# Spectra of the hyena filters in a two-layer trunk: 256 samples summed at 256 frequencies, and the same from even and odd samples at 128 frequencies

## The chip, the cores and the metric

One NeuronCore of one Trainium2 chip runs the whole kernel. The metric is the time of one execution on the device in microseconds (us); a profile gives the span from the first to the last instruction of one profiled execution.

## What is computed

The reference is a trunk of two layers over 256 tokens of 2048 channels in float32, with 256 context tokens. Layer 0 is attention (two kinds of heads) and a gated convolutional feed-forward part; layer 1 is a Hyena long convolution of order 2 and again a feed-forward part. Every sub-layer is preceded by an RMS norm with a scale and a shift that come from a conditioning vector (the modulation). What the change touches is the Hyena filters and the long convolution with them:

```python
hf = (a @ f_w3).reshape(L, HY_ORDER, 2, D_MODEL)          # a: a sine network of the position, L = 256
filt = hf * decay[:, None, None, :]

def _bidir_long_conv(u, h_fwd, h_bwd, d_skip):
    filt = concatenate([h_fwd, zeros((1, D)), h_bwd[:0:-1]], axis=0)
    filt = filt / sum(abs(filt), axis=0, keepdims=True)
    n = 2 * L
    y = irfft(rfft(u, n=n, axis=1) * rfft(filt, n=n, axis=0)[None], n=n, axis=1)[:, :L]
    return y + u * d_skip
```

There are two orders, so 2 x 2 x 2048 filters of 256 samples. They do not depend on the tokens.

## The kernel before, in words

Every large product is made of three matmuls (`mm3`, lines 319 to 322): both operands are split into a high part, rounded to the float32r type by ScalarE (L315 for weights, L325 for other tiles), and a low part, the difference by VectorE (L316, L326). TensorE (PE) computes high x high (L320), and the two mixed products (L321, L322, in the order in which they are called). Weights are read in tiles of 256 rows x 512 columns (512 KB), through a pool of 6 raw buffers and 3 pairs of split buffers; the DMAs are issued on SyncE's queue (SP).

**Order of the work.** The program is written as generators. `drive` (L300) steps a main stream and after each step gives shares of steps to background streams. A scheduler then sets the order of each engine's instructions from the order in which they were recorded and from priorities; an engine runs its instructions in that order.

**The start** (up to about 181 us). The scale and shift vectors of the first norm are products of the conditioning vectors with 33.5 MB of weights. `ada_block(g)`, g from 0 to 3, makes 512 columns of both (L871: PE reads the raw weights; L875 to L883 turn the sums into columns), and the first projection of the attention keys and values (label kv0) follows it block by block, since each block lets another quarter of the normed tokens be computed (`Normed.get`, L379). Beside them, `bg.step(START_RATE)` steps the generators `filter_net` and `filters` for the first two of four groups of 512 channels (`DCS`, L173).

**`filters`** (L526) makes, for each group of channels and each order, the samples (`samples`: L546 PE, L548 VectorE times the decay, L325/L326 split, L550 absolute values, L555 to L560 the norm) and then the spectra (`spectra`, L563). The samples' tile `layers` holds forward + backward and forward - backward; their cosine and sine sums are the two halves of a spectrum at the 256 frequencies f + 1/2. A sum over 256 samples at 128 frequencies takes two tiles of samples (tt) and so 2 x 3 matmuls of 128 x 512 into one bank; ScalarE scales the bank into the tile `so` (L572); after both frequency tiles of a half a DMA on ScalarE's queue (L574) writes the half to memory. So each (order, channel group) has 24 matmuls, 4 ScalarE passes and 4 steps (`yield`). There are 8 of them: 4 in the start, 2 in the fill of the attention's output projection, 2 in that of the first down projection.

**The fills.** `fill` (L1091) runs the samples of one more channel group beside the last pass of a projection back into the stream. Then the kernel has to wait: the norm of the next sub-layer needs the sums of squares of the finished stream, by a chain of L352 (PE sums), L354 (VectorE), L331 and L332 (VectorE, first guess of a root), L334 to L344 (GpSimd, Newton steps), L360 (ScalarE), L361 (PE), L388 (VectorE), L393 (ScalarE), and only then the next sub-layer's matmuls. `main_done` and `fill_steps` (L1101, L1109) put the remaining steps of the spectra there: `GAP = 3, 5` steps before the chain is recorded and after it, and the rest of the steps (up to 40) after the first normed group. The chain runs at high priority. There are three such gaps: before the first feed-forward part (about 700 to 713 us), before the Hyena layer (about 1523 to 1536 us), both with fill, and before the second feed-forward part (about 1975 to 1985 us), without.

**The modulation of later sub-layers** is computed by VectorE during everything (L434, L436: 128 x 1024 products, from `araw` tiles through two buffers), so VectorE's queue now and then waits for such a DMA with other work behind it.

In the start the filters take their banks from a ring of two banks (6 and 7), in the fills from a ring of four.

## Time and profile before

| | |
|---|---|
| time, median of 3 runs | 2727.53 us (2714.11 to 2729.07) |
| span of the profiled execution | 2722.9 us; the profile gives no time outside it |
| TensorE (PE) busy | 2588.1 us, 95%, 19638 matmuls |
| VectorE (DVE) busy | 1931.1 us, 71%, 2581 instructions |
| ScalarE (ACT) busy | 1267.0 us, 47%, 1810 instructions |
| GpSimd (POOL) busy | 35.1 us, 1% |
| memory traffic | 639.97 MB, mean 235 GB/s |
| mean granted clock of TensorE | 0.986 of full speed |

A group of instructions of the page gives line, engine, operation, output <- inputs, shapes, count, then busy time and the mean of one in ns. Matmuls overlap (the next enters the array while the last one leaves), so the duration of one is longer than the distance between two. The chain that ended last consists of PE for 60% and of DMA for 18%, of which 16% are the `araw` transfers of the modulation.

### The profile page before, as it was taken

What the parts mean: (1) busy time and instruction counts of PE and PEld (TensorE: products, weight loads), DVE (VectorE), ACT (ScalarE), POOL (GpSimd) and SP (SyncE); (2) the same over time, 40 slices, a digit from 0 to 9 for tenths busy, and PEclk for the clock granted to TensorE, in tenths of its full rate; (3) what the DMA queues carried; (4) which work ended last, traced back from release to release, by engine and by line L of the source; (5) the groups of instructions that cost most, each with busy time, mean ns of one, the idle gap of its engine ahead of it and who ended that gap; (6) DMA issues with size and microseconds to landing.
All of it is one profiled execution on the core that took longest, in us unless ns stands there. A gap on an engine that the chain in (4) does not pass through costs nothing.

```text
span 2722.9 us, 48064 instructions
## 1 busy us (share of the span) xinstructions
PE 2588.1 (95%) x19638; PEld 2371.2 (87%) x19638; DVE 1931.1 (71%) x2581; ACT 1267.0 (47%) x1810; POOL 35.1 (1%) x146
## 2 busy tenths in 40 slices
PE   6999999989999999999899999998989999999999
PEld 2567776678889999999898899998989999999999
DVE  6557668688877777768778778888777655556564
ACT  3542235655544343445444555554454444445543
POOL 0000001000000000000000000000000000000000
PEclk8999999999999999999999999999989999999999
DMA  8887785278698989878897865555579666666664
GB/s 309 311 308 240 229 273 182 86 236 267 217 307 273 300 283 312 270 244 292 292 302 261 274 196 179 170 178 186 169 233 310 203 195 192 194 193 195 194 208 141
DMA packets 282628, 639.97 MB, mean 235 GB/s; under 512 B 19783, under 2 KB 19880, under 8 KB 282408
## 3 DMA queue, kind: packets, MB, share of 16 engines
q1 hardware_dynamic: 280104, 628.53, 71.8%
q10 hardware_dynamic: 2304, 8.39, 0.8%
q8 instruction: 153, 2.51, 0.4%
q14 instruction: 67, 0.55, 0.1%
HBM read 624.25 MB, written 12.58 MB: 234 GB/s over the span
## 4 chain that ended last, share of the span: by engine, by line
PE 60%; DMA 18%; DVE 13%; issue 5%; ACT 2%; POOL 1%; SPq 1%; DVEq 0%; ACTq 0%; POOLq 0%
DMA araw_ada<-ada_w 16%; PE ps_proj L322 6%; PE ps_proj L321 6%; PE ps_proj L320 5%; DVE aacc_ada L436 4%; PE ps_hy L322 3%; PE ps_hy L321 3%; PE ps_hy L320 3%; DVE wlo_proj L316 2%; DMA raw_proj<-wd 1%; PE ps_ada L871 1%; PE ps_kv L320 1%; PE ps_kv L322 1%; PE ps_kv L321 1%; PE ps_ada L320 1%
## 5 line engine op out<-in xcount | busy, mean ns | idle before, releaser
L436 DVE SCALAR_TENSOR_TENSOR aacc_ada<-araw_ada,slat,aacc_ada 128x1024 f32<-128x1024 f32 x300 | 384.7, 1282 | 236.9 <-DMA araw_ada<-ada_w 236.3
L322 PE MATMUL ps_proj<-ph,wlo_proj 128*128 128x256 f32 x1408 | 391.6, 280 | 18.2 <-DVE wlo_proj L316 18.1
L320 PE MATMUL ps_proj<-ph,whi_proj 128*128 128x256 f32 x1408 | 391.5, 279 | 3.7 <-ACT whi_proj L315 2.2
L315 ACT CAST whi_proj<-raw_proj 128x1024 fp32r<-128x1024 f32 x240 | 251.3, 1052 | 302.3 <-PE ps_proj L321 273.6
L321 PE MATMUL ps_proj<-pl,whi_proj 128*128 128x256 f32 x1408 | 390.7, 278 | 1.3 <-DVE pl L326 1.3
L316 DVE TENSOR_TENSOR wlo_proj<-raw_proj,whi_proj 128x1024 fp32r<-128x1024 f32 x240 | 291.9, 1221 | 116.6 <-ACT whi_proj L315 116.3
L322 PEld LDWEIGHTS ps_proj<-ph,wlo_proj 128*128 128x128 f32 x1408 | 264.6, 189 | 24.7 <-DVE wlo_proj L316 22.3
L320 PEld LDWEIGHTS ps_proj<-ph,whi_proj 128*128 128x128 f32 x1408 | 265.4, 189 | 7.4 <-ACT whi_proj L315 2.9
L321 PEld LDWEIGHTS ps_proj<-pl,whi_proj 128*128 128x128 f32 x1408 | 266.1, 189 | 3.0 <-DVE pl L326 2.3
L320 PE MATMUL ps_hy<-hhi,whi_hy 128*128 128x256 f32 x768 | 215.8, 282 | 1.1 <-ACT hhi L393 1.1
L321 PE MATMUL ps_hy<-hlo,whi_hy 128*128 128x256 f32 x768 | 215.2, 280 | 0.6 <-DVE hlo L395 0.6
L322 PE MATMUL ps_hy<-hhi,wlo_hy 128*128 128x256 f32 x768 | 214.8, 280 | 0.0
L315 ACT CAST whi_hy<-raw_hy 128x1024 fp32r<-128x1024 f32 x96 | 100.8, 1059 | 115.3 <-PE ps_hy L321 104.9
L321 PEld LDWEIGHTS ps_hy<-hlo,whi_hy 128*128 128x128 f32 x768 | 146.3, 190 | 2.2 <-DVE hlo L395 0.8
L320 PEld LDWEIGHTS ps_hy<-hhi,whi_hy 128*128 128x128 f32 x768 | 144.9, 189 | 2.5 <-ACT hhi L393 1.3
L322 PEld LDWEIGHTS ps_hy<-hhi,wlo_hy 128*128 128x128 f32 x768 | 145.1, 189 | 0.8 <-DVE wlo_hy L316 0.7
L316 DVE TENSOR_TENSOR wlo_hy<-raw_hy,whi_hy 128x1024 fp32r<-128x1024 f32 x96 | 116.3, 1220 | 24.5 <-ACT whi_hy L315 24.1
L320 PE MATMUL ps_kv<-whi_kv,hhi 128*128 128x512 f32 x256 | 102.8, 402 | 9.0 <-ACT KTb L749 6.2
L322 PE MATMUL ps_kv<-whi_kv,hlo 128*128 128x512 f32 x256 | 101.7, 397 | 0.0
L321 PE MATMUL ps_kv<-wlo_kv,hhi 128*128 128x512 f32 x256 | 101.3, 396 | 0.0
L315 ACT CAST whi_kv<-raw_kv 128x1024 fp32r<-128x1024 f32 x40 | 41.9, 1051 | 101.8 <-PE ps_kv L322 82.2
L320 PE MATMUL ps_proj<-oh,whi_proj 128*128 128x256 f32 x256 | 75.0, 297 | 2.2 <-DVE hf L548 1.2
(9846 smaller groups left out, 7973.2 us busy)
## 6 DMA issues: line engine op xcount, KB each, us to landing
araw_ada<-ada_w SPq DMA_DIRECT2D x320, 512.0 KB, 5.1
raw_proj<-wd SPq DMA_DIRECT2D x176, 512.0 KB, 4.5
raw_hy<-hw_in SPq DMA_DIRECT2D x96, 512.0 KB, 4.6
raw_ada<-ada_w SPq DMA_DIRECT2D x46, 512.0 KB, 6.8
raw_kv<-w_in SPq DMA_DIRECT2D x40, 512.0 KB, 4.8
raw_q<-w_in SPq DMA_DIRECT2D x32, 512.0 KB, 4.6
raw_proj<-w_out SPq DMA_DIRECT2D x32, 512.0 KB, 4.8
raw_proj<-hw_out SPq DMA_DIRECT2D x32, 512.0 KB, 4.0
```

What stands on the lines that cost most here:

```text
L315: A.copy(hi, raw)
L316: V.tensor_tensor(lo, raw, hi, op=ALU.subtract)
L320: PE.matmul(o, lh, rh, start=first, stop=False, **kw)
L321: PE.matmul(o, lh, rl, start=False, stop=False, **kw)
L322: PE.matmul(o, ll, rh, start=False, stop=last, **kw)
L436: V.scalar_tensor_tensor(out=a, in0=raw, scalar=slat[:, kt:kt + 1], in1=a, op0=ALU.mult, op1=ALU.add)
L871: PE.matmul(pv[32 * q:32 * q + 32], sl[:, 2 * i + q], raws[q // 2][:, q % 2], start=i == 0, stop=i == 6, tile_position=(0, 32 * q))
```

## The change

Frequencies f (even, 0 to 254) are now paired with 255 - f instead of standing beside the odd ones in rising order. Samples are stored even ones first, then odd ones, so that a tile of samples is one parity. At frequency 255 - f the even samples give the same sum up to a sign and the odd samples the other sign. `spectra` therefore makes per half only two sums at 128 frequencies, over the even tile (`pe`) and the odd tile (`po`), and forms both frequency tiles as their sum and difference: ScalarE scales `pe` into a new tile `e`, VectorE makes two `scalar_tensor_tensor` passes from `po` and `e`. Only the first 128 frequencies stand in the table, so `k_fg` is 512 columns narrower and `split_const` loads and splits one piece less at each of the three calls of `filters`. A half is one step now, not two. The comments were taken out too, which is left out here, and three lines added ahead of `spectra`, so that L320 to L322 are L323 to L325 below, L352 is L355, L354 is L357, L361 is L364, L436 is L439, L871 is L877.

```diff
-    fo = np.concatenate([np.arange(0, L, 2), np.arange(1, L, 2)])[None, :]
+    fo = np.concatenate([np.arange(0, L, 2), L - 1 - np.arange(0, L, 2)])[None, :]
     t = np.arange(L)[:, None]
-    ph = np.pi * ((t * (2 * fo + 1)) % (2 * n)) / n
-    fmat = np.concatenate([np.cos(ph), np.sin(ph)], axis=1).reshape(2, P, 512).transpose(1, 0, 2).reshape(P, 1024)
+    eo = np.concatenate([np.arange(0, L, 2), np.arange(1, L, 2)])
+    ph = np.pi * ((eo[:, None] * (2 * fo[:, :P] + 1)) % (2 * n)) / n
+    fmat = np.concatenate([np.cos(ph), np.sin(ph)], axis=1).reshape(2, P, 2 * P).transpose(1, 0, 2).reshape(P, 512)
...
-        "k_tab": tab, "k_fg": fg, "k_z": np.ascontiguousarray(z.T),
-        "k_decay": np.ascontiguousarray(decay.reshape(2, P, D).transpose(1, 0, 2)),
+        "k_tab": tab, "k_fg": fg, "k_z": np.ascontiguousarray(z[eo].T),
+        "k_decay": np.ascontiguousarray(decay[eo].reshape(2, P, D).transpose(1, 0, 2)),
...
-        fh, fl = (t.rearrange("p (t f) -> p t f", t=2) for t in split_const(0, 1024, "f"))
+        fh, fl = (t.rearrange("p (t f) -> p t f", t=2) for t in split_const(0, 512, "f"))
...
                 so = q4([P, 2, 512], F32, "spo")
                 xh, xl = hl[2 * half], hl[2 * half + 1]
-                for f in range(2):
-                    p = ftag[0]()
-                    for tt in range(2):
-                        c = slice(half * T + f * P, half * T + (f + 1) * P)
-                        mm3(p, fh[:, tt, c], fl[:, tt, c], xh[:, tt], xl[:, tt], tt == 0, tt == 1)
-                    A.activation(so[:, f], p, AF.Copy, scale=1.0 / (2 * T))
-                    yield
+                c = slice(half * P, (half + 1) * P)
+                pe, po = ftag[0](), ftag[0]()
+                mm3(pe, fh[:, 0, c], fl[:, 0, c], xh[:, 0], xl[:, 0], True, True)
+                mm3(po, fh[:, 1, c], fl[:, 1, c], xh[:, 1], xl[:, 1], True, True)
+                e = s2([P, 512], F32, "se")
+                A.activation(e, pe, AF.Copy, scale=1.0 / (2 * T))
+                V.scalar_tensor_tensor(out=so[:, 0], in0=po, scalar=1.0 / (2 * T), in1=e, op0=ALU.mult, op1=ALU.add)
+                V.scalar_tensor_tensor(out=so[:, 1], in0=po, scalar=(half * 2 - 1) / (2 * T), in1=e, op0=ALU.mult,
+                                       op1=ALU.subtract if half else ALU.add)
+                yield
                 A.dma_start(spec[o][dc][:, 2 * half:2 * half + 2], so)
...
-    dh, dl = split_const(1024, 512, "d")
-    ih, il = split_const(1536, 512, "i")
+    dh, dl = split_const(512, 512, "d")
+    ih, il = split_const(1024, 512, "i")
```

With half the steps per spectrum the generators come to their ends earlier, and the scheduler sets another order. Three places follow.

**TensorE's order in the first gap, the last rows ahead of the sum of the norm (L361, now L364)**, before. `ps_fill` are the banks of the spectra, `ps_proj` with `ones` those of the norm:

```order
L320 MATMUL ps_fill_6001<-fhl_5683,fh_5478 128x512
L321 MATMUL ps_fill_6001<-fhl_5684,fh_5478 128x512
L322 MATMUL ps_fill_6001<-fhl_5683,fl_5479 128x512
L321 MATMUL ps_fill_6009<-fhl_5684,fh_5478 128x512
L322 MATMUL ps_fill_6009<-fhl_5683,fl_5479 128x512
L320 MATMUL ps_fill_6009<-fhl_5683,fh_5478 128x512
L321 MATMUL ps_fill_6009<-fhl_5684,fh_5478 128x512
L322 MATMUL ps_fill_6009<-fhl_5683,fl_5479 128x512
L361 MATMUL ps_proj_1292_5985<-s_5986,ones_67 128x128 x2
```

The same place with the change:

```order
L325 MATMUL ps_fill_5916<-fhl_5643,fl_5443 128x512
L355 MATMUL ps_proj_1301_5928<-ones_67,sqacc_4171 128x1
L355 MATMUL ps_proj_1301_5928<-ones_67,sq_5862 128x1
L355 MATMUL ps_proj_1301_5928<-ones_67,sq_5865 128x1
L355 MATMUL ps_proj_1301_5928<-ones_67,sq_5892 128x1
L355 MATMUL ps_proj_1301_5928<-ones_67,sq_5895 128x1
L355 MATMUL ps_proj_1301_5928<-ones_67,sqacc_4171 128x1
L355 MATMUL ps_proj_1301_5928<-ones_67,sq_5862 128x1
L355 MATMUL ps_proj_1301_5928<-ones_67,sq_5865 128x1
L355 MATMUL ps_proj_1301_5928<-ones_67,sq_5892 128x1
L355 MATMUL ps_proj_1301_5928<-ones_67,sq_5895 128x1
L364 MATMUL ps_proj_1306_5956<-s_5957,ones_67 128x128 x2
```

Before, 26 matmuls of spectra stood between the last sum of squares and L361; now none does: all 12 that are left in this gap stand ahead of the sums. In the second gap 3 stand behind the sums, where 22 stood, and 6 more of before, which stood among the Hyena layer's first matmuls, are gone.

**VectorE's order in the first gap, from the norm's first instruction (L354, now L357) to the first product with it (L388, now L391)**, before:

```order
L354 TENSOR_SCALAR t_5968<-ps_proj_1287_5957 128x2
L316 TENSOR_TENSOR wlo_ffn0.0_1313_6104<-raw_ffn0.0_1311_6101,whi_ffn0.0_1312_6103 128x1024
L331 TENSOR_SCALAR t_5971<-t_5968 128x2
L436 SCALAR_TENSOR_TENSOR aacc_ada_1405_6871<-araw_ada_1417_6968,slat_84,aacc_ada_1405_6871 128x1024
L332 TENSOR_SCALAR t_5970<-t_5971 128x2
L436 SCALAR_TENSOR_TENSOR aacc_ada_1405_6871<-araw_ada_1422_7007,slat_84,aacc_ada_1405_6871 128x1024
L388 TENSOR_TENSOR ht_6020<-xs_4199,ps_proj_1292_5985 128x256 x3
```

And with the change:

```order
L357 TENSOR_SCALAR t_5939<-ps_proj_1301_5928 128x2
L576 SCALAR_TENSOR_TENSOR spo_5900<-ps_fill_5902,se_5909 128x512
L334 TENSOR_SCALAR t_5942<-t_5939 128x2
L577 SCALAR_TENSOR_TENSOR spo_5900<-ps_fill_5902,se_5909 128x512
L335 TENSOR_SCALAR t_5941<-t_5942 128x2
L576 SCALAR_TENSOR_TENSOR spo_5914<-ps_fill_5916,se_5923 128x512
L577 SCALAR_TENSOR_TENSOR spo_5914<-ps_fill_5916,se_5923 128x512
L439 SCALAR_TENSOR_TENSOR aacc_ada_1415_6815<-araw_ada_1420_6849,slat_84,aacc_ada_1415_6815 128x1024
L439 SCALAR_TENSOR_TENSOR aacc_ada_1415_6815<-araw_ada_1427_6912,slat_84,aacc_ada_1415_6815 128x1024
L391 TENSOR_TENSOR ht_5964<-xs_4163,ps_proj_1306_5956 128x256 x3
```

Inside the norm's chain (up to L332, now L335) two passes of 128 x 1024 have given way to two of 128 x 512. In the second gap the two passes of 128 x 1024 there (both L436) give way to two of 128 x 512 in the same manner.

**TensorE's order in the last modulation block of the start** (L871, now L877: products with the raw weights), before:

```order
L871 MATMUL ps_ada_260_1110<-raw_ada_261_1111,sl 32x512
L320 MATMUL ps_filters_1091<-fhl_858,fh_293 128x512
L321 MATMUL ps_filters_1091<-fhl_859,fh_293 128x512
L322 MATMUL ps_filters_1091<-fhl_858,fl_294 128x512
L320 MATMUL ps_filters_1091<-fhl_858,fh_293 128x512
L321 MATMUL ps_filters_1091<-fhl_859,fh_293 128x512
L322 MATMUL ps_filters_1091<-fhl_858,fl_294 128x512
L871 MATMUL ps_ada_260_1110<-raw_ada_261_1111,sl 32x512
L871 MATMUL ps_ada_260_1110<-raw_ada_262_1113,sl 32x512 x2
```

And with the change:

```order
L884 MATMUL ps_ada_270_1092<-sel_109,adast_1090 128x2 x4
L877 MATMUL ps_ada_271_1101<-raw_ada_272_1102,sl 32x512 x2
L877 MATMUL ps_ada_271_1101<-raw_ada_273_1104,sl 32x512 x2
L323 MATMUL ps_ada_121_448<-whi_kv_275_1112,hhi_1028 128x512
L323 MATMUL ps_ada_122_449<-whi_kv_275_1112,hhi_1028 128x512
L323 MATMUL ps_ada_123_450<-whi_kv_275_1112,hhi_1042 128x512
L323 MATMUL ps_ada_124_451<-whi_kv_275_1112,hhi_1042 128x512
```

Of the 96 spectra matmuls of the start, 24 stood among the products of the second block, 24 of the third and 48 of the last; of the 48 that are left 15, 33 and none, the last of them ahead of the last block's first product.

## Rows read from the trace of the kernel before

**Rows 1.** Engines by stretch: length, busy (count) of PE, PEld, DVE, ACT, POOL; clock, DMA share, GB/s.
```profile
75.00:100.00 25.00, 25.00 (x124) 16.31 (x123) 10.74 (x22) 10.68 (x20) 0.00 (x0) 1.00 0.77 272
100.00:125.00 25.00, 24.54 (x125) 13.24 (x120) 11.47 (x24) 11.83 (x24) 0.00 (x0) 1.00 0.97 342
125.00:150.00 25.00, 24.14 (x128) 15.39 (x128) 11.15 (x24) 14.51 (x30) 0.00 (x0) 1.00 0.96 331
150.00:170.00 20.00, 18.87 (x84) 11.72 (x84) 6.44 (x10) 8.95 (x18) 0.00 (x0) 0.91 0.96 341
...
670.00:730.00 60.00, 54.29 (x359) 48.55 (x359) 50.91 (x95) 37.17 (x70) 2.92 (x10) 0.94 0.57 182
```

**Rows 2.** What SyncE's DMA queue waited for, 60 to 200 us: total, times, longest.
```profile
SPq L309 <- PE ps_ada L871: 69.6, 22, 9.2
```

**Rows 3.** Instructions on the spectra's banks: count, ns min/median/max, first and last start.
```profile
L320 PE MATMUL ps_filters<-fhl,fh x32: 389/397/507, 74.7 to 160.5; 128*128 128x512 f32 x32
...
L548 DVE TENSOR_TENSOR hf<-ps_filters,dec x16: 679/688/693, 38.3 to 127.2; 128x512 f32<-128x512 f32 x16
```

**Rows 4.** Order in time on PE in the start: start, duration, instruction. First, seventh from it.
```profile
80.36 0.40 PE L320 MATMUL ps_filters<-fhl,fh 128*128 128x512 f32 x1
...
81.75 0.40 PE L322 MATMUL ps_ada<-whi_kv,hlo 128*128 128x512 f32 x1
```

**Rows 5.** The same at the start's end: last modulation product, then kv0 matmuls.
```profile
161.29 1.06 PE L871 MATMUL ps_ada<-raw_kv,sl 128*32 128x512 f32 x8
...
165.74 0.63 PE L322 MATMUL ps_ada<-whi_kv,hlo 128*128 128x512 f32 x1
...
168.30 0.63 PE L322 MATMUL ps_ada<-whi_kv,hlo 128*128 128x512 f32 x1
```

**Rows 6.** Order in time on DVE in the first gap, the norm's chain.
```profile
704.50 0.16 DVE L354 TENSOR_SCALAR t<-ps_proj 128x2 f32<-128x2 f32 x1 [1.98 <-PE ps_proj L352]
...
705.79 1.28 DVE L436 SCALAR_TENSOR_TENSOR aacc_ada<-araw_ada,slat,aacc_ada 128x1024 f32<-128x1024 f32 x1
706.99 0.16 DVE L332 TENSOR_SCALAR t<-t 128x2 int32<-128x2 int32 x1
```

**Rows 7.** Order in time on PE in the first gap and behind it.
```profile
710.08 0.39 PE L322 MATMUL ps_fill<-fhl,fl 128*128 128x512 f32 x1
711.45 0.78 PE L361 MATMUL ps_proj<-s,ones 128*128 128x128 f32 x4 [0.98 <-ACT s L360]
...
715.22 0.41 PE L322 MATMUL ps_ffn0.0_1303_6039<-hhi,wlo_ffn0.0_1307_6044 128*128 128x256 f32 x1
...
718.42 0.32 PE L320 MATMUL ps_ffn0.0_1301_6037<-hhi,whi_ffn0.0_1309_6073 128*128 128x256 f32 x1
```

**Rows 8.** DVE in the second gap, the norm's chain.
```profile
1528.02 0.16 DVE L354 TENSOR_SCALAR t<-ps_proj 128x2 f32<-128x2 f32 x1 [1.72 <-PE ps_proj L352]
...
1530.62 0.16 DVE L332 TENSOR_SCALAR t<-t 128x2 int32<-128x2 int32 x1
```

**Rows 9.** PE behind the second gap: first and last of 6 late spectra matmuls.
```profile
1554.51 0.47 PE L320 MATMUL ps_fill<-fhl,fh 128*128 128x512 f32 x1 [0.47 <-DVE ht L388]
...
1555.74 0.39 PE L322 MATMUL ps_fill<-fhl,fl 128*128 128x512 f32 x1
```

**Rows 10.** PE in the third gap, without fill, and behind it.
```profile
1982.82 1.22 PE L361 MATMUL ps_proj<-s,ones 128*128 128x128 f32 x4 [5.03 <-ACT s L360]
...
1985.19 0.58 PE L320 MATMUL ps_ffn1.0_3360_20704<-hhi,whi_ffn1.0_3365_20710 128*128 128x256 f32 x1 [1.15 <-ACT hhi L393]
...
1991.59 0.32 PE L321 MATMUL ps_ffn1.0_3361_20705<-hlo,whi_ffn1.0_3368_20740 128*128 128x256 f32 x1
```

**Rows 11.** PE by stretches of 1 us there: length, busy (count), clock, DMA share, GB/s.
```profile
1978.00:1979.00 1.00, 0.00 (x0) 0.51 0.72 180
...
1990.00:1991.00 1.00, 1.00 (x7) 0.50 0.00 0
```

**Rows 12.** DVE in the start: the longest wait for a modulation tile.
```profile
158.53 1.28 DVE L436 SCALAR_TENSOR_TENSOR aacc_ada<-araw_ada,slat,aacc_ada 128x1024 f32<-128x1024 f32 x1 [11.61 <-DMA araw_ada<-ada_w]
```

## Prediction

> **What bounds the kernel now.** I read the engines' totals first: TensorE is busy for 95% of the span, so it is the engine whose work counts, but what an instruction less on it is worth has to be read where that instruction stands. The change takes 12 of 24 matmuls from each of 8 spectra. By the lists of the instructions on the spectra's banks [rows 3] 96 of the 192 stood in the start, the rest in the fills: in the out-projection and first down projection themselves, and in the two gaps behind these.
>
> In the start the windows [rows 1] show TensorE without a pause from 75 to 150 us, and DMA at 0.77 of its engines in the first 25 us and at 0.96 to 0.97 after that. SyncE's queue waits 22 times, 69.6 us in all, for TensorE to be done with a raw tile of the modulation [rows 2]. So both limits lie near each other: fewer matmuls free raw tiles sooner, the DMA runs ahead, and is then full itself. In the gaps VectorE, GpSimd and ScalarE make the root of the norm one after the other, and TensorE can only fill. VectorE's order in time [rows 6, 8] shows two passes on other data inside that chain; TensorE's order [rows 7, 9, 10] shows what follows the gap, and at which clock.
>
> **The sum.** It is made against the profiled execution, span 2722.9 us, for which the profile gives no time outside the span. The median of the runs, 2727.53, is 4.6 above it, and I add that at the end.
>
> **Start.** 48 matmuls go. One lasts 397 ns [rows 3], but they overlap: from the first to the seventh start of a run [rows 4] it is 81.75 - 80.36 = 1.39 us for six, 0.232 us each. 48 x 0.232 = 11.1 us less work for TensorE; that is the upper end. The DMA caps it: from 75 to 161 us the windows [rows 1] moved 25 x 272 + 25 x 342 + 25 x 331 + 11 x 341 kB/us, together 27.4 MB. At 342 kB/us throughout that takes 80.1 us, not 86: 5.9 can be had. I take this value, as the queue's waits [rows 2] show that TensorE, not memory, is what holds the transfers up in the first stretch, and the 0.97 that nothing holds them up after it. Against it stands the clock. The last block's products lose all spectra between them, so TensorE will pause there for tiles. The trace shows what follows pauses: behind the last product at 161.29 us, where the stretch's clock falls to 0.91 in the mean, the 6 spacings between the matmuls at 165.74 and 168.30 are 0.43 us each [rows 5], not 0.23. I add one more such stretch of 8 matmuls, 8 x 0.2 = 1.6. Start: -5.9 + 1.6 = **-4.3**; ends -11.1 and 0.
>
> The Trainium skill (page "TensorE: Matmul & The Clock Gate", section "Back-to-back issue gap") gives 131 ns for a matmul of 512 columns in a sustained stream of weight loads and matmuls. By it the 48 would be worth 6.3 us, not 11.1; the spacing in this trace is 232 ns [rows 4], so the measurement decides, and the DMA's cap lies below either.
>
> **First gap.** VectorE's chain from its first instruction at 704.50 to the root's guess at 706.99 is 2.49 us, since two passes of 128 x 1024, 1.28 each, stand in it [rows 6]. In the new order two of 128 x 512 stand there. The trace has no such `scalar_tensor_tensor`; the nearest row of that size and engine, a product of 0.688 us that reads a bank too [rows 3], is what I take. Its ends are 0.64, half of the 1.28, and 1.28 itself. 2.49 - 2 x 0.69 = 1.1 less. Ahead of the sums 12 spectra matmuls stand now for 10 before (36 in all, 26 behind): at most 2 x 0.23 = 0.5 us later, which I count as nothing, as VectorE's squares feed the sums meanwhile. Against that no matmul is left to run behind the sums, where 26 stood: the last of them ended at 710.5, 1 us before the norm's broadcast (L361) at 711.45 [rows 7]. TensorE will stand idle as in the third gap, where the clock is at 0.51 while it idles, the broadcast waited 5.03 us and took 1.22 where the first gap's took 0.78, and the clock is still at 0.50 at 1990 [rows 10, 11]. With fill the matmuls that take 0.41 reach from 715.22 to the first of 0.32 at 718.42 [rows 7], 3.2 us, half of which, 1.6, is lost. Without, they reach from 1985.19 to 1991.59 [rows 10], 6.4 us: 3.2 lost, and 0.4 on the broadcast. So the clock makes the gap 3.2 + 0.4 - 1.6 = 2.0 dearer. Sum: -1.1 + 2.0 = **+0.9**; ends -1.1 and +2.0.
>
> **Second gap.** The chain takes 2.60 us with two passes of 128 x 1024 in it [rows 8], so the same edit gives -1.2. Six spectra matmuls that stood late, behind the gap, waited 0.47 and took 6 x 0.23 [rows 9]: -1.9. Three matmuls of fill are left behind the sums of 22, and I take the first gap's 2.0 for the clock here too. Sum: -1.2 - 1.9 + 2.0 = **-1.1**; ends -3.1 and +2.0.
>
> **At nothing, with their cover.** 32 passes on VectorE at about 0.69 are 22 us. In the start VectorE is busy for 11 of 25 us, in the out-projection for 50.9 of 60 [rows 1], where 4 of them come; without that cover they cost 2.8. 16 scaling passes of as many columns leave ScalarE, which is busy for 11 to 15 of 25 us [rows 1] and not the bound either. Three times one constant piece (256 KB, a rounding, a subtraction) is not loaded; the two later ones lie beside TensorE's stream, the first is 0.256 MB, under 1 us of DMA at 342. The DMA that stores a half now follows VectorE's two passes on ScalarE's queue, with roundings of weights behind it; both banks of the start's ring of two are held for the same time. The two passes take 1.4 us a half, and 16 halves lie between 74.7 and 160.5 [rows 3], one in 5.4 us; I take 0, and what it costs when a pass is late is a rival.
>
> Total -4.3 + 0.9 - 1.1 = **-4.5**: span 2718.4, median 2723.0.
>
> **Rivals.** (A) *Everything goes through.* The transfers of the start speed up by as much as TensorE does, and the gaps, shorter by their chains, leave the clock as it was: -11.1 - 1.1 - 3.1 = -15.3, 2712.2 us. For it: SyncE's waits [rows 2]; against it: 0.97 [rows 1]. Chance 0.20.
>
> (B) *The clock takes all.* Every microsecond at half clock counts, idle or not: in the third gap 1978.0 to 1991.6, half of 13.6, is 6.8 [rows 10, 11], 3.2 more than the 3.6 I took, in both gaps; and the start's pause costs the 3.2 us of its cold row in full, twice the 1.6 [rows 5]. -4.5 + 6.4 + 1.6 = +3.5, 2731.0 us. For it: the third gap, at half clock from its middle until 1991.59 [rows 10, 11]. Against it: over half of these 13.6 us TensorE only waits for the chain, which does not run on its clock. Chance 0.10. The Trainium skill (same page, section "HAM oscillation — how this bites in real kernels") reckons the penalty of a throttled stretch as half of its time. By it this rival would be the likeliest; that only matmuls pay is my reading of the rows, and no run here shows yet which holds.
>
> (C) *Slower: VectorE's new passes stand behind a modulation tile.* Products of the modulation wait in VectorE's order for their transfer, once for 11.61 us [rows 12]. In the new order such a product stands ahead of a spectrum's passes at two places of the start. Before, only ScalarE released a spectrum's bank; now VectorE does, so the ring of two stops TensorE, and the store's issue holds up ScalarE's roundings. It decides if the wait is longer than the matmuls that TensorE still has ahead in its order. Both in full: 2 x 11.6 - 4.5 = +18.7, 2746.2 us. For it: the start's DMA is full, so such tiles come late; against it: the row stands at the very end of the start, and earlier waits are shorter. Chance 0.10.
>
> **How the numbers follow.** The forecast, 2723.0, has 0.60. A measurement of this kernel can tell some 0.5% from no change, 13.6 us of 2727.53. The forecast and B lie inside; A lies 1.7 us beyond the bound, and with a few of the forecast's own outer cases I give it 0.18 as faster; C is beyond the other, and a little of it falls short. Faster 0.18, the same 0.74, slower 0.08. The range: the ends of the terms are -11.1 - 1.1 - 3.1 = -15.3 and 0 + 2.0 + 2.0 + 2.8 = +6.8, so 2712.2 to 2734.3. The runs shown lie 15 us apart (2714.11 to 2729.07), so a median of a few may lie some 2 or 3 us off: 2709 to 2737. That takes in A and B and leaves out C, and little else.
>
> **What would show it.** Right: the last modulation product ends 4 to 6 us earlier, with DMA above 0.95 from 75 us on; the chain in the first gap is 1.4 us from L357 to L335, in the second also; the broadcast L364 comes after a pause of TensorE at half clock. Wrong: the start's end does not move (DMA or VectorE holds it), a spectrum's pass waits for a modulation tile while TensorE's matmuls on the other bank wait for it, or the pauses of the gaps leave the clock at 1.00.

## The result and the profile after the change

The changed kernel takes 2749.59 us (median of 4 runs, 2744.02 to 2753.70) where before takes 2726.52 (4 runs, 2714.11 to 2729.07): ratio 1.0096, 95% interval 1.0067 to 1.0125, that is 23 us between the medians and 26 by the ratio. The forecast was 2723.0, its range ended at 2737.0. The profiled execution has a span of 2742.2 us, 19.3 more than before's.

To see where, I read the starts of the same products in TensorE's order in time in both traces: the last kv0 product of the start, the first and last product of a projection, the first product behind a gap. The start ends at 191.2 us where it ended at 182.3; the out-projection takes 158.0 us instead of 152.1, the first gap 14.4 instead of 13.2, the down projection of the first layer 301.5 instead of 290.6, the second gap 15.7 instead of 13.8. So +8.9, +5.9, +1.2, +10.9 and +1.9; some 9.5 us come back in the other stretches, which move by as much between two traces of before. *Cold* below is TensorE at a granted clock of 0.50 (1.2 GHz) where it has 1.00 (2.4 GHz) otherwise.

**The start.** Windows of the changed kernel, columns as in [rows 1]:

```profile
75.00:100.00 25.00, 24.27 (x100) 13.92 (x101) 14.63 (x23) 11.39 (x21) 0.00 (x0) 0.93 0.77 266
100.00:125.00 25.00, 22.72 (x111) 11.95 (x110) 15.21 (x30) 11.28 (x23) 0.00 (x0) 1.00 0.87 314
125.00:150.00 25.00, 22.47 (x109) 12.19 (x109) 9.96 (x17) 9.67 (x21) 0.00 (x0) 1.00 0.86 319
150.00:170.00 20.00, 17.31 (x72) 8.00 (x72) 4.85 (x12) 2.22 (x4) 0.00 (x0) 0.74 0.73 254
```

DMA falls from 0.96 and more to 0.87, 0.86 and 0.73, and TensorE idles too. SyncE's queue, the instructions on the spectra's banks, and TensorE in the last block:

```profile
SPq L312 <- PE ps_ada L877: 65.5, 25, 9.8
```
```profile
L323 PE MATMUL ps_filters<-fhl,fh x16: 393/452/796, 72.9 to 136.2; 128*128 128x512 f32 x16
L576 DVE SCALAR_TENSOR_TENSOR spo<-ps_filters,se x8: 686/692/694, 83.4 to 137.1; 128x512 f32<-128x512 f32 x8
L577 DVE SCALAR_TENSOR_TENSOR spo<-ps_filters,se x8: 680/681/684, 84.0 to 137.7; 128x512 f32<-128x512 f32 x8
```
```profile
151.29 3.28 PE L877 MATMUL ps_ada<-raw_ada,sl 128*32 128x512 f32 x8 [2.88 <-DMA raw_ada<-ada_w]
155.25 1.87 PE L884 MATMUL ps_ada<-sel,adast 128*128 128x2 f32 x8 [0.69 <-ACT adast L881]
157.05 1.93 PE L877 MATMUL ps_ada<-raw_ada,sl 128*32 128x512 f32 x8
...
170.06 1.05 PE L884 MATMUL ps_kv<-sel,adast 128*128 128x2 f32 x8 [0.78 <-ACT adast L881]
```

The spectra's last sum starts at 136.2, not at 160.5 [rows 3]. Behind it TensorE has only modulation products and kv0 products, in lumps. From 143.2 it uses the loaded raw tiles in a row, then waits 2.88 us for the next, with DMA full, and turns cold: eight modulation products, four at a time, take 1.93 us (157.05) where they took 1.06 [rows 5]. From 161.7 to 166.6 twenty kv0 products run in one go; no raw tile comes free meanwhile, and DMA pauses. The two windows, columns as above:

```profile
148.00:152.00 4.00, 1.12 (x4) 0.18 (x4) 3.30 (x5) 2.01 (x6) 0.00 (x0) 0.78 1.05 394
164.00:168.00 4.00, 4.00 (x28) 2.32 (x29) 0.00 (x0) 0.00 (x0) 0.00 (x0) 1.00 0.18 68
```

SyncE still waits for TensorE, 65.5 us in all [rows 2: 69.6].

**The first gap.** VectorE and then GpSimd in order of time:

```profile
716.64 0.16 DVE L357 TENSOR_SCALAR t<-ps_proj 128x2 f32<-128x2 f32 x1 [1.73 <-PE ps_proj L355]
716.72 0.68 DVE L576 SCALAR_TENSOR_TENSOR spo<-ps_fill,se 128x512 f32<-128x512 f32 x1
717.31 0.16 DVE L334 TENSOR_SCALAR t<-t 128x2 int32<-128x2 int32 x1
717.38 0.69 DVE L577 SCALAR_TENSOR_TENSOR spo<-ps_fill,se 128x512 f32<-128x512 f32 x1
717.98 0.16 DVE L335 TENSOR_SCALAR t<-t 128x2 int32<-128x2 int32 x1
718.05 0.69 DVE L576 SCALAR_TENSOR_TENSOR spo<-ps_fill,se 128x512 f32<-128x512 f32 x1
...
719.24 2.60 DVE L439 SCALAR_TENSOR_TENSOR aacc_ada<-araw_ada,slat,aacc_ada 128x1024 f32<-128x1024 f32 x2
```
```profile
718.28 0.19 POOL L337 TENSOR_TENSOR t<-t 128x2 f32<-128x2 f32 x1 [155.68 <-DVE t L335]
...
719.38 1.19 POOL L341 TENSOR_TENSOR t<-t 128x2 f32<-128x2 f32 x1
720.65 1.24 POOL L342 TENSOR_TENSOR t<-t,t 128x2 f32<-128x2 f32 x1
721.99 0.19 POOL L344 TENSOR_SCALAR t<-t 128x2 f32<-128x2 f32 x1
```

The chain on VectorE is 1.34 us long, 1.15 less than before [rows 6], as forecast. But the two modulation products now run beside GpSimd's steps, and each makes one of those last 1.2 us instead of 0.19. Before, only one step in this gap was so long and none in the second. TensorE:

```profile
715.57 1.03 PE L355 MATMUL ps_proj<-ones,sq 128*128 128x1 f32 x8
723.53 1.22 PE L364 MATMUL ps_proj<-s,ones 128*128 128x128 f32 x4 [6.92 <-ACT s L363]
725.89 0.58 PE L323 MATMUL ps_ffn0.0_1311_5981<-hhi,whi_ffn0.0_1316_5987 128*128 128x256 f32 x1 [1.15 <-ACT hhi L396]
...
730.37 0.35 PE L324 MATMUL ps_ffn0.0_1313_5983<-hlo,whi_ffn0.0_1316_5987 128*128 128x256 f32 x1
```

It idles for 6.92 us ahead of the broadcast [rows 7: 0.98], which takes 1.22 [rows 7: 0.78], and products stay cold from 725.89 to 730.37.

**The out-projection.** VectorE, and the product that waits for it:

```profile
702.80 0.68 DVE L577 SCALAR_TENSOR_TENSOR spo<-ps_fill,se 128x512 f32<-128x512 f32 x1
...
703.73 0.68 DVE L576 SCALAR_TENSOR_TENSOR spo<-ps_fill,se 128x512 f32<-128x512 f32 x1
704.33 0.68 DVE L577 SCALAR_TENSOR_TENSOR spo<-ps_fill,se 128x512 f32<-128x512 f32 x1
704.93 1.22 DVE L319 TENSOR_TENSOR wlo_proj<-raw_proj,whi_proj 128x1024 fp32r<-128x1024 f32 x1
```
```profile
706.20 0.39 PE L325 MATMUL ps_proj<-oh,wlo_proj 128*128 128x256 f32 x1 [2.57 <-DVE wlo_proj L319]
706.42 0.28 PE L323 MATMUL ps_proj<-oh,whi_proj 128*128 128x256 f32 x1
...
709.66 0.41 PE L323 MATMUL ps_proj<-oh,whi_proj 128*128 128x256 f32 x1
```

The spectra's passes stand ahead of the low part of the last weights. TensorE waits 2.57 us and is cold soon after, from 706.6 to 710.0 (0.41 a product where 0.28 is the rule).

**The down projection.** A queue behind a modulation tile. VectorE, ScalarE, TensorE:

```profile
1475.60 0.75 DVE L437 TENSOR_SCALAR aacc_ada<-araw_ada,slat 128x1024 f32<-128x1024 f32 x1 [1.34 <-DMA araw_ada<-ada_w]
1476.27 0.69 DVE L551 TENSOR_TENSOR hf<-ps_fill,w 128x512 f32<-128x512 f32 x1
```
```profile
1476.99 0.62 ACT L328 CAST fhl<-hf 128x512 fp32r<-128x512 f32 x1 [2.36 <-DVE hf L551]
1477.51 1.04 ACT L328 CAST ph<-prod 128x1024 fp32r<-128x1024 f32 x1
```
```profile
1478.61 0.80 PE L323 MATMUL ps_proj<-ph,whi_proj 128*128 128x256 f32 x2 [4.41 <-ACT ph L328]
...
1537.63 0.58 PE L325 MATMUL ps_proj<-ph,wlo_proj 128*128 128x256 f32 x1 [3.20 <-DVE wlo_proj L319]
```

A modulation product (L437) waits for its transfer, the filter's samples (`hf`) stand behind it, ScalarE's rounding of them waits, and behind that stands the rounding of `ph`, which TensorE needs: 4.41 us, then a cold stretch. No spectrum is in this row yet: these are samples, whose instructions the change does not touch. Before has the same wait, shorter:

```profile
1463.74 0.50 PE L320 MATMUL ps_proj<-ph,whi_proj 128*128 128x256 f32 x2 [1.42 <-ACT ph L325]
```

### The profile page after: what moved, and what is told of

Same layout as the page of the kernel before. It is cut to its first block, busy times and chain, and to the rows that moved or that the text cites. A ratio compares the mean times of both kernels' runs of the same rounds, so it can differ in the third digit from the quotient of the medians.

```text
span 2742.2 us, 47887 instructions
## 1 busy us (share of the span) xinstructions
PE 2592.5 (95%) x19542; PEld 2370.3 (86%) x19542; DVE 1950.7 (71%) x2610; ACT 1256.5 (46%) x1791; POOL 37.9 (1%) x146
## 4 chain that ended last, share of the span: by engine, by line
PE 61%; DMA 19%; DVE 12%; issue 5%; ACT 2%; POOL 1%; SPq 1%; DVEq 0%; POOLq 0%; ACTq 0%
DMA araw_ada<-ada_w 16%; PE ps_proj L325 6%; PE ps_proj L323 6%; PE ps_proj L324 6%; DVE aacc_ada L439 3%; PE ps_hy L324 3%; PE ps_hy L325 3%; PE ps_hy L323 3%; DVE wlo_proj L319 2%; PE ps_ada L877 1%; DMA raw_proj<-wd 1%; DMA raw_ada<-ada_w 1%; PE ps_kv L323 1%; PE ps_kv L325 1%; PE ps_kv L324 1%
## 5 line engine op out<-in xcount | busy, mean ns | idle before, releaser
L439 DVE SCALAR_TENSOR_TENSOR aacc_ada<-araw_ada,slat,aacc_ada 128x1024 f32<-128x1024 f32 x300 | 385.0, 1283 | 223.0 <-DMA araw_ada<-ada_w 222.4
L325 PE MATMUL ps_proj<-ph,wlo_proj 128*128 128x256 f32 x1408 | 393.5, 281 | 18.8 <-DVE wlo_proj L319 18.5
L323 PE MATMUL ps_proj<-ph,whi_proj 128*128 128x256 f32 x1408 | 394.6, 281 | 7.1 <-ACT ph L328 4.4
L319 DVE TENSOR_TENSOR wlo_proj<-raw_proj,whi_proj 128x1024 fp32r<-128x1024 f32 x240 | 292.3, 1222 | 120.5 <-ACT whi_proj L318 120.4
L325 PEld LDWEIGHTS ps_proj<-ph,wlo_proj 128*128 128x128 f32 x1408 | 266.5, 190 | 26.2 <-DVE wlo_proj L319 24.8
L323 PEld LDWEIGHTS ps_proj<-ph,whi_proj 128*128 128x128 f32 x1408 | 267.1, 190 | 12.2 <-ACT ph L328 5.2
L323 PE MATMUL ps_hy<-hhi,whi_hy 128*128 128x256 f32 x768 | 215.8, 282 | 1.1 <-ACT hhi L396 1.1
L325 PE MATMUL ps_hy<-hhi,wlo_hy 128*128 128x256 f32 x768 | 214.5, 280 | 0.0
L323 PEld LDWEIGHTS ps_hy<-hhi,whi_hy 128*128 128x128 f32 x768 | 144.8, 189 | 2.6 <-ACT hhi L396 1.4
L325 PEld LDWEIGHTS ps_hy<-hhi,wlo_hy 128*128 128x128 f32 x768 | 145.2, 189 | 0.7 <-DVE wlo_hy L319 0.7
L319 DVE TENSOR_TENSOR wlo_hy<-raw_hy,whi_hy 128x1024 fp32r<-128x1024 f32 x96 | 116.6, 1222 | 23.5 <-ACT whi_hy L318 23.0
L323 PE MATMUL ps_kv<-whi_kv,hhi 128*128 128x512 f32 x256 | 101.9, 399 | 8.2 <-ACT KTb L755 6.1
L325 PE MATMUL ps_kv<-whi_kv,hlo 128*128 128x512 f32 x256 | 101.3, 396 | 0.0
L323 PE MATMUL ps_proj<-oh,whi_proj 128*128 128x256 f32 x256 | 76.6, 303 | 2.6 <-DVE xs L980 1.0
```

The costliest lines, as they stand in the source:

```text
L319: V.tensor_tensor(lo, raw, hi, op=ALU.subtract)
L323: PE.matmul(o, lh, rh, start=first, stop=False, **kw)
L325: PE.matmul(o, ll, rh, start=False, stop=last, **kw)
L439: V.scalar_tensor_tensor(out=a, in0=raw, scalar=slat[:, kt:kt + 1], in1=a, op0=ALU.mult, op1=ALU.add)
```

## Experiments

Ratios are to before in the same comparison (4 runs of it beside the changed kernel, 16 to 26 beside the others, medians 2724.0 to 2727.1). Stages in us, from TensorE's order in time of each profiled execution, as above:

| kernel | start's end | out-proj. | gap 1 | down proj. | gap 2 | ratio (95%) |
|---|---|---|---|---|---|---|
| before | 182.3 | 152.1 | 13.2 | 290.6 | 13.8 | 1 |
| before_again | 180.0 | 151.0 | 13.2 | 289.2 | 14.0 | |
| changed | 191.2 | 158.0 | 14.4 | 301.5 | 15.7 | 1.0096 (1.0067, 1.0125) |
| after_again | 195.0 | 155.0 | 14.6 | 300.8 | 15.5 | |
| e1_start_only | 195.7 | 152.1 | 13.2 | 292.0 | 13.8 | 1.0068 (1.0045, 1.0090) |
| e2_fills_only | 181.4 | 154.8 | 14.6 | 298.6 | 15.5 | 1.0036 (1.0018, 1.0055) |
| e3_four_start | 184.1 | 155.2 | 15.6 | 296.8 | 16.0 | 1.0085 (1.0053, 1.0118) |
| e4_rate | 186.2 | 153.7 | 15.8 | 300.8 | 16.5 | 1.0058 (1.0024, 1.0092) |
| e7_start_kept | 176.8 | 154.2 | 13.2 | 290.4 | 13.8 | 1.0004 (0.9985, 1.0023) |
| e6_fills_wide | 180.3 | 154.9 | 14.6 | 289.4 | 15.5 | 1.0039 (1.0016, 1.0061) |
| e13_no_dve | 180.5 | 148.5 | 14.4 | 288.7 | 14.5 | 1.0001 (0.9978, 1.0024) |
| e15_narrow_no_dve | 178.8 | 154.3 | 13.9 | 297.3 | 13.2 | 1.0029 (1.0012, 1.0045) |
| e10_gap12 | 179.8 | 157.8 | 13.9 | 290.2 | 15.9 | 1.0051 (1.0033, 1.0069) |
| e11_one_more | 179.5 | 154.2 | 13.9 | 294.0 | 15.9 | 1.0052 (1.0031, 1.0072) |
| e8_all_kept | 180.7 | 155.0 | 15.7 | 295.5 | 15.2 | 1.0049 (1.0031, 1.0066) |
| e12_all_kept_gap | 181.3 | 156.5 | 14.0 | 291.4 | 16.0 | 1.0050 (1.0028, 1.0072) |
| e14_all_kept_g13 | 178.3 | 153.6 | 14.0 | 295.2 | 15.8 | 1.0019 (0.9995, 1.0042) |

**How far a stage moves by itself.** Both kernels once more.

> The kernel before once more, to see how far the stages of one execution move by themselves: the end of kv0 (182.1), the last product of the out-projection (700.3) and of the down projection (1522.4) should lie within 3 us; where they move by more, differences of that size between single traces tell nothing.

> The changed kernel once more, for its stages: kv0's end 7 to 11 us later than before's 182, the first gap's L364 after 5 us or more of idle, and 7 to 10 us lost in the down projection between 1457 and 1522 of before; where one of these is missing, it isn't the change's.

Over the eight traces with before's start it ends between 178.8 and 182.3, so before's own trace is at the upper end. The named losses come again in the changed kernel. Stretches that wait for the modulation move by 5 us and more (from the first gap to the down projection: 518.3 and 523.6 in before), and the single runs of before lie between 2711 and 2740 us: totals need many runs, and stages are compared over short stretches.

**Which half.** One half of the change at a time, `spare` being true in the start; the half that stays as before loads its constant in two pieces, as before did:

```diff
+                if not (spare):        # e2: if not (not spare)
+                    for f in range(2):
+                        p = ftag[0]()
...
+                        A.activation(so[:, f], p, AF.Copy, scale=1.0 / (2 * T))
+                        yield
```

> The new spectra in the start alone; the fills make theirs as before the change, from a wide table of all frequencies over the even-odd samples. Theory P (pacing): the filter work of the start comes to its end before the last modulation block, TensorE then waits for transfers and turns cold; the first projection (kv0) ends about 8.8 us later than before, and of it 5 to 7 us are left at the end: 2732 to 2735 us. Theory F (all the loss is made in the fills, by VectorE's new passes and the earlier end of the fill, and the start's lag would be caught up later): within 3 us of before, 2727. Both: the out-projection, the down projection and the gaps as before (first gap idle about 1 us ahead of the norm's broadcast, not 6.9).

> The new spectra in the fills alone; the start makes them as before. Theory F: the out-projection with its gap loses some 7 us and the down projection with its gap some 10 to 13, total 2740 to 2747 us, and the start ends at 182 us as before. Theory P: the loss is the start's, so 2727 to 2732. If the two halves are independent, this run's loss and that of the run with the new spectra in the start alone add up to 23 us.

Both lose, 0.68% and 0.36%, and the sum is the whole change's 0.96% within the intervals. Neither theory alone holds. In the first run the start's lag, 13 to 15 us, is not caught up later: the total loses 18 us by the ratio, 6 either way, where P had 5 to 7 left at the end. In the second the down projection has 8 us of the loss, and it has them in its last 100 us, where the samples are made.

**The start.** Four steps to a spectrum instead of two, or a lower rate:

```diff
-                mm3(po, fh[:, 1, c], fl[:, 1, c], xh[:, 1], xl[:, 1], True, True)
                 e = s2([P, 512], F32, "se")
                 A.activation(e, pe, AF.Copy, scale=1.0 / (2 * T))
+                if spare:
+                    yield
+                mm3(po, fh[:, 1, c], fl[:, 1, c], xh[:, 1], xl[:, 1], True, True)
```
```diff
-START_RATE = 1.2
+START_RATE = 0.9
```

> All of the change, but in the start a spectrum is given in four steps again (one step per sum of three matmuls), so that it is spread over as many steps of the main stream as before. The same matmuls and the same VectorE passes. Theory P: the start's filters reach further into the last modulation block, kv0 ends 4 to 9 us earlier than with the change (182 to 187 us instead of 191), total 2741 to 2746. Theory V (VectorE's passes or their releasing of the banks hold the start up): kv0 ends at 191 us or later, total 2749 to 2752.

> All of the change with START_RATE 0.9 instead of 1.2: all filter work of the start is slowed, samples too, 24 steps for 32 before. Theory P: as the run with four steps, kv0 ends 4 to 9 us earlier than with the change, total 2741 to 2746. Theory V: no gain, 2749 to 2752.

With four steps the start ends at 184.1 with the same matmuls and the same passes on VectorE: P (pacing) holds for the stage, and V (VectorE's passes hold it up) falls there. The lower rate gives 186.2: its modulation products end 3.7 us before before's, but then TensorE waits 1.47 and 4.54 us for the split halves of a kv0 weight, as VectorE's queue has a modulation product with a late tile ahead of the low part. The totals hardly show either gain (their intervals are 0.6% wide, and that of the four steps, 2749.2 us, lies where V put it); both runs have the fills' losses. Then four steps and the constant in two pieces, spectra of the fills as before (here and in the later runs with four steps the second bank is taken behind the `yield`, not ahead of it):

```diff
-        fh, fl = (t.rearrange("p (t f) -> p t f", t=2) for t in split_const(0, 512, "f"))
+        fh, fl = (t.rearrange("p (t f) -> p t f", t=2) for t in split_const(1536, 1024, "f"))
```

> New spectra in the start alone, with the constant in two pieces and four steps to a spectrum, the fills as before. Theory P: kv0 ends within 2 us of before (182 us), and the total is within 5 us of before, as 48 matmuls less on TensorE buy nothing where transfers set the pace. Theory D (the start does gain once its order is kept): kv0 ends 4 to 6 us earlier, total 2719 to 2723. If kv0 ends 8 us or more later, VectorE's passes or banks hold the start up.

Its windows from 100 to 170 us:

```profile
100.00:125.00 25.00, 24.98 (x120) 13.42 (x117) 15.09 (x30) 13.01 (x26) 0.00 (x0) 1.00 0.92 339
125.00:150.00 25.00, 22.68 (x102) 11.50 (x101) 9.42 (x21) 8.66 (x18) 0.00 (x0) 1.00 0.86 315
150.00:170.00 20.00, 17.40 (x84) 12.40 (x83) 8.91 (x27) 12.16 (x22) 0.00 (x0) 0.91 0.94 348
```

1.0004: nothing lost, nothing gained. The start ends at 176.8 here, which alone would fit D, and between 178.3 and 181.3 in the three runs of the whole change with the same start (below), about 179.3 in the mean against 180.3 in the eight traces with the old start. So 48 matmuls less, 11.1 us of TensorE, are worth about 1 us, no more than these ends scatter. TensorE is idle for 2.3 to 2.6 us in each of the last two windows: its time was not what the start lacked. With two steps the change's starts end 11 to 15 us behind that 180.3, with four steps alone 4 us (184.1); the rest goes with the second piece and the bank's place, which were not tested apart.

**The fills.** First the constant in two pieces there too, which leaves each engine's order up to the first spectrum of a fill as before. (Half the columns of each piece are read by nothing; the text on record says the second piece.) Then VectorE's passes left out, with either constant; ScalarE writes both halves of the stored tile, which then holds the two sums and not the spectrum:

```diff
-                e = s2([P, 512], F32, "se")
-                A.activation(e, pe, AF.Copy, scale=1.0 / (2 * T))
-                V.scalar_tensor_tensor(out=so[:, 0], in0=po, scalar=1.0 / (2 * T), in1=e, op0=ALU.mult, op1=ALU.add)
...
+                A.activation(so[:, 0], pe, AF.Copy, scale=1.0 / (2 * T))
+                A.activation(so[:, 1], po, AF.Copy, scale=1.0 / (2 * T))
```

> As the run with the new spectra in the fills alone, but the constant is still loaded and split in two pieces (the second is read by nothing), so that each engine's order up to the first spectrum of a fill is that of before. Theory O (order: one constant piece less shifts all that the fill places after it against the modulation's products and the weights, and VectorE's queue then waits for a modulation tile with the filter's product behind it): the down projection, which lost 8 to 9 us between 1460 and 1522 in the runs with the narrow constant, loses at most 2, total 2724 to 2730. Theory V (VectorE's two new passes per half and the emptier gap are what costs): no change against the narrow run, the down projection loses 8 again, total 2732 to 2740.

> New spectra in the fills alone with the constant in two pieces, but VectorE's sum and difference are left out there: ScalarE scales both banks into the two halves of the stored tile, so the stored spectra of half the channels are the even and odd sums themselves, not the spectra. TensorE's matmuls, ScalarE's passes and the DMAs are as many as in the run with the constant in two pieces. Theory V (what is left of the fills' loss, 10 us, is VectorE's 32 half-size passes ahead of the weights' low parts and inside the gaps): the out-projection from 650 to 700 loses 1 us or less where it lost 2 to 5, total 2722 to 2729. Theory K (the emptier gap, that is idle and cold): the total stays at 2732 to 2738 and the gaps are as long (14.6 and 15.5 us from the last product to the next sub-layer's first).

> New spectra in the fills alone with the narrow constant, and VectorE's sum and difference left out there (as in the run with the constant in two pieces): each engine's order ahead of the spectra is that of the changed kernel, only the passes are gone. Theory O: the 8 us that the down projection loses between 1457 and 1503 come from the shifted order alone, so they are there without the passes, and the total is 2728 to 2734 (1.001 to 1.004). Theory V alone: the passes cause them; gone here, 2722 to 2728.

(Without the passes ScalarE has two passes a half, as in before; in the wide run it has one, not as many, as the text on record has it.)

The down projection takes 298.6 us with the narrow constant, that is with one piece, and 289.4 with the wide one (before: 289.2 to 290.6); without VectorE's passes it takes 297.3 and 288.7. The last 100 us of it, the same 612 products in e2_fills_only and then e6_fills_wide, columns as in [rows 1]:

```profile
1428.20:1530.80 102.60, 90.16 (x659) 82.09 (x659) 82.36 (x91) 40.85 (x51) 0.00 (x0) 0.93 0.80 265
1433.50:1523.90 90.40, 84.65 (x659) 77.38 (x659) 74.92 (x86) 41.21 (x51) 0.00 (x0) 1.00 0.83 280
```

TensorE idles for 6.7 us more and its clock is lower (the 200 us ahead differ by 3 us the other way). So the 8 us come from the order that shifts when one piece of a constant is not loaded, with or without the passes: O (order) holds. The other traces agree: in all six with the narrow constant in this fill these products take 99 to 103 us, with a wait for `ph` of 3.7 to 5.3 us; in the eleven others they take 90 to 95, and that wait is 3.1 at most. The rest is VectorE's passes: without them and with the old order the ratio is 1.0001, the out-projection 148.5. The wait that does it, in the wide run and as in the changed kernel, VectorE and TensorE (L588 and L589 are L576 and L577, L321 is L319, L327 is L325):

```profile
694.00 0.68 DVE L588 SCALAR_TENSOR_TENSOR spo<-ps_fill,se 128x512 f32<-128x512 f32 x1
694.60 0.68 DVE L589 SCALAR_TENSOR_TENSOR spo<-ps_fill,se 128x512 f32<-128x512 f32 x1
695.20 1.21 DVE L321 TENSOR_TENSOR wlo_proj<-raw_proj,whi_proj 128x1024 fp32r<-128x1024 f32 x1
```
```profile
696.47 0.58 PE L327 MATMUL ps_proj<-oh,wlo_proj 128*128 128x256 f32 x1 [2.66 <-DVE wlo_proj L321]
```

Without the passes this wait is not there; two of 1.2 to 1.3 us some ten us earlier, which before has too, are. All eleven traces with the passes in this fill have it, with 1.95 to 2.67 us; the six without have none above 0.49 in the last 8 us. In the traces with the narrow constant in this fill another wait for `wlo_proj`, 2.26 to 2.29 us, stands some 45 us before the end, with the passes or without: the shifted order costs in the out-projection too (154.3 for 148.5 without passes). The narrow constant is not alone in that: the two gap runs below have 2.7 us there with the wide one. The gaps are nearly as long and as empty without the passes (14.4 and 14.5 us), TensorE ahead of the first broadcast:

```profile
709.68 1.23 PE L366 MATMUL ps_proj<-s,ones 128*128 128x128 f32 x4 [6.66 <-ACT s L365]
```

That run has no loss, so K, that idle and cold time in the gaps is what is left of the fills' loss, falls as the whole cause. The gaps' own +1.2 and +0.7 us are still there; the out-projection, 2.5 to 3.6 us shorter than in before, makes up for them. What does not close: the wide constant repaired the down projection but not the total (1.0039 against 1.0036). The order alone costs 0.29%, the passes alone 0.39%, both together 0.36% and not 0.68%; with the intervals of all three, each about 0.2% either way, that they add up is just possible, and that they do is not shown.

**The gaps.** Fewer steps ahead of the sums of the norm, then one more step behind them:

```diff
-    fill_steps(GAP[0])
+    fill_steps(1)        # second gap: 2
```

> New spectra in the fills alone with the constant in two pieces, and GAP[0] 1 in the first gap and 2 in the second (3 before): 6 of the 12 spectra matmuls of the first gap, and 6 where 3 were in the second, now stand behind the sums of the norm, and the sums are spread between the matmuls ahead, not in a row. Theory K (with the sums all behind the fill, and nothing behind them, a gap starts later and TensorE goes idle and cold): the first gap with its approach, which cost 5 us, gives back 2 to 4, total 2727 to 2731. Theory V (VectorE's passes in the gap and the projections): no gain, 2733 to 2738.

> As the run before it in this list, with one more step of six matmuls in each fill, behind the spectra, whose bank nothing reads: 12 matmuls stand behind the sums in both gaps, so that TensorE is idle for 1.4 us less ahead of the norm's broadcast. Nothing else is added. Theory K: the clock is held a little longer and the total lies 0 to 3 us below the run without; if idle time and clock don't matter, the same within 2 us or, as 12 more matmuls, up to 3 us above.

The first gap is 0.7 us shorter (13.9 for 14.6). The sums are done 1.5 us earlier, but three of GpSimd's steps are long now, for two. The total is no better (1.0051), but that says nothing on K: all three runs with 2 in the second gap (e12 below is the third) lose 8 us in the first 30 us of the Hyena layer. The six matmuls more, 1.0052 for 1.0051, change nothing that these runs can tell; the idle time ahead of the broadcast fell by 0.4 us in the first gap and rose by 0.7 in the second. VectorE and TensorE of e10_gap12 in the Hyena layer:

```profile
1543.21 2.59 DVE L441 SCALAR_TENSOR_TENSOR aacc_ada<-araw_ada,slat,aacc_ada 128x1024 f32<-128x1024 f32 x2
1545.72 0.68 DVE L331 TENSOR_TENSOR il<-fgt,ih 128x512 fp32r<-128x512 f32 x1
1546.33 1.40 DVE L393 TENSOR_TENSOR ht<-xs,ps_proj 128x256 f32<-128x256 f32 x4
```
```profile
1548.21 0.39 PE L325 MATMUL ps_hy<-hhi,whi_hy 128*128 128x256 f32 x1 [2.76 <-ACT hhi L396]
1554.29 0.55 PE L325 MATMUL ps_hy<-hhi,whi_hy 128*128 128x256 f32 x1 [3.64 <-DVE ht L393]
```

Two modulation products came ahead of the norm's product (`ht`), and TensorE waits for it twice. A few matmuls moved by one place cost more than all that they could fill.

**The whole change with its order kept.** Wide constant, four steps, and the gaps as before, as in the last pair, and with 1 and 3:

> The whole change, but with the constant in two pieces and four steps to a spectrum in the start. Theories O and P: most of the 23 us come back, total 2724 to 2732. Theory V: 2740 or more.

> The whole change with the constant in two pieces, four steps to a spectrum in the start, and GAP[0] 1 and 2: the version of the change that all findings point to. Theories O, P and K together: 2724 to 2730, no worse than before and not better, since the start is held by transfers and the gaps by the norm's chain. Theory V: 2735 or more.

> The whole change with the constant in two pieces, four steps to a spectrum in the start, and GAP[0] 1 in the first gap and 3, as before the change, in the second. All three runs with 2 in the second gap lost 8 us in the first 30 us of the Hyena layer (two modulation products and a spectrum's pass came ahead of its norm on VectorE). If that is an accident of the order and not of the spectra, it is gone here: 2727 to 2731, within 0.3% of before. If the loss is the spectra's own, 2735 to 2738 as with 2.

1.0049 and 1.0050, and 1.0019 (0.9995 to 1.0042) with 1 and 3. The 8 us in the Hyena layer are gone with the second gap's setting put back: they were an accident of the order. So about half, and in the last version most, of the loss comes back without one matmul more, and that version can't be told from before. It differs from the first of the three by the first gap's setting alone: that gap is 1.7 us shorter (14.0 for 15.7) and the ratio 0.3% lower, with intervals that overlap. So a cost of the first gap is not excluded, and whether its setting gives more than the 1.7 us stays open. No version was faster; the down projection still takes 295 us in two of the three, so their orders are not free of such waits.

## Why the prediction was wrong

Its forecast was -4.5 us and 0.74 for no change; measured +23 to +26. Two steps failed: the start, -4.3, lost 9 to 13 us, and the fills' new order and passes, put at nothing, lost 8 to 11 us in the down projection and 3 to 6 in the out-projection. The rival that ended slower had +18.7, almost the size, by luck and not by its mechanism: the one product in the start that waits for a modulation tile stands at 148.70 us and waits 2.98 us, 11 us behind the last spectrum's pass.

- *"5.9 can be had"* (start). The step that failed. It took 342 kB/us as what nothing holds up and asked only how many matmuls went, not where the remaining ones stand. The windows show 254 to 319, and the runs why: at an unchanged rate of steps, half the steps per spectrum end the filters' work 24 us earlier. (342 was no ceiling either: 394 from 148 to 152 us.) With the steps kept (and the wide constant) the 48 matmuls give about 1 us. The price per matmul, 0.232, was right and decided nothing. The text had seen that the last block would have no spectra, and charged that with 1.6 us; the stage lost 9 to 13.
- *"Three times one constant piece is not loaded"*, at nothing. The work is nothing, its place is not: in the fill of the down projection it moves all that follows against the modulation's products, 8 us of that stage, with and without the passes.
- *"At nothing, with their cover"* (VectorE's passes). The cover was read off VectorE's busy 50.9 of 60 us, and the bound of 2.8 us without it is four passes at 0.69. The cost is a wait of 2.6 us at one place, at the end of the projection, and the cold stretch behind it; that 2.8 is near is luck. The fills without the passes are 0.38% faster (1.0001 for 1.0039). A busy share says nothing on what stands behind an instruction in its queue.
- *First gap, +0.9.* Near in size (+1.9) by parts that were not: VectorE's chain -1.15 (forecast -1.1), but GpSimd's +1.1, the sums +0.9 (forecast "at most 0.5", counted as nothing: all ten now stand in a row behind the matmuls), the broadcast +0.4 as forecast, and behind it cold products for 4.5 us instead of 3.2, that is +0.6 (forecast 1.6).
- *Second gap, -1.1.* The gap itself +1.9: sums +1.0, VectorE's chain -1.3, GpSimd's +1.8 (two long steps where there was none), broadcast +0.4. The -1.9 for the six late matmuls behind it came: the Hyena layer's lag against before falls by 2.1 us where they stood, from 22.8 to 20.6.
- *Rival B, the clock.* The gaps bear out that only matmuls pay: with 6.92 us of idle at half clock the clock costs 0.4 + 0.6 more than before, not the 2.0 + 3.2 of this rival. The Trainium skill ("TensorE: Matmul & The Clock Gate", section "HAM oscillation — how this bites in real kernels") reckons the penalty as half of the throttled time. By it the first gap's clock would cost 4.9 us more, an estimate: it is at 0.50 from 717 to 730 us here and from 715.2 to 718.4 in before, and half of that is 6.5 and 1.6. The trace does not agree: the parts above come to 1.0. The total of the run with empty gaps and no passes, 1.0001, can't decide it, as its interval reaches 6 us either way.

## What to carry to other kernels

Removing work from an engine in a statically ordered program moves everything behind it. Price the new order at the few places where an in-order queue has a late transfer in it (here the modulation's tiles on VectorE), and look for what stands behind that instruction, before pricing the work itself. When background work is dealt out in steps, halving the steps of a piece is a change of pace; keep the steps, or the place where the work ends, and test the two apart by leaving what does no harm in place (here one constant piece and one `yield`).

## What the hardware showed unexpectedly

GpSimd's step of the norm on a 128 x 2 tile takes 0.19 us, but 1.03 to 1.28 over all traces when VectorE runs a pass beside it that reads two tiles of SBUF (the modulation product, 719.24 above, or a weight's low part). Beside VectorE's new passes, which read a bank and one tile, GpSimd's stays at 0.19 (the step at 718.28, beside a pass that begins at 718.05). Over the gaps of all traces GpSimd's ten steps take 2.7 us with no long one, 3.7 with one, 4.5 to 4.8 with two and 5.5 to 5.6 with three. So a pass taken out of VectorE's part of the chain was given back in GpSimd's. The Trainium skill (page "GPSIMD Engine Reference", section "Specifications") says that GpSimd shares its interfaces to SBUF with VectorE and contends with VectorE's instructions that have two SBUF inputs; this trace agrees, and gives the size, about 1 us a step. Read beforehand, it spoke against taking the gain on VectorE's chain as a gain of the gap.
